# Small experts multiply gate and up tiles in float32 on two halves of the array's columns, with eleven raw tiles

## The chip, the core and the metric

One core of one Trainium2 chip runs the whole program. The time is device microseconds (us) from the first to the last instruction of the program and what lies around it, a median of three runs. TensorE is called PE here, its weight loads PEld, VectorE DVE, ScalarE ACT, GpSimd POOL, and SP is the engine that issues nearly all DMAs.

## What is computed

The reference is a decoder trunk of two layers over 272 tokens of width 1024. Each layer mixes tokens (attention, a state-space branch and a short convolution) and then applies a channel mixer. The second layer's channel mixer is the part that matters here, a choice of two experts out of eight for each of the last 256 tokens:

```
def swiglu(t, w_gu, w_down):
    gate, up = jnp.split(t @ w_gu, 2, axis=-1)
    return (jax.nn.silu(gate) * up) @ w_down

logits = (t @ router_w + router_b)
top_val, top_idx = lax.top_k(logits, TOP_K)          # TOP_K = 2, N_EXPERTS = 8
top_w = jax.nn.softmax(top_val, axis=-1)
for e in range(N_EXPERTS):
    out = out + combine[:, e:e + 1] * swiglu(t, w_gu[e], w_down[e])
```

Each expert has gate and up weights of 1024 x 7168 and down weights of 3584 x 1024, all float32. Every expert's weights are read once from memory, however many tokens it has.

## The kernel before

**Tiles and steps.** An expert is done in 7 steps (`NJ`); step `j` takes 512 columns of gate and of up and 512 rows of down. The weights of a step are six raw tiles of 128 x 2048 float32, 1 MB each: two of gate, two of up, two of down. `expert_units` (line 1230) lists these units in the order in which they are loaded and used: gate 0 and 1 of step i, down 0 and 1 of step i-2, up 2 and 3 of step i. Gate and up are both called `up` in the code. There are 8 x 7 x 6 = 336 units.

**Raw tiles.** `load_unit` (line 1244) issues the DMA of the next unit on SP into the next of ten raw tiles, which come from two pools A and B in the order of `RAWS`. A tile can be written again when all readers of the unit before it in that tile are done. The DMAs stand in one queue, in the order of the units. The first eleven units are asked for ahead of the loop, and each call of `make_low(k)` asks for one more.

**Splitting.** To multiply float32 with the array's faster one-pass format (float32r), a unit is split into a high and a low part: `make_high` (line 1270) copies it on ACT with rounding, `make_low` (line 1282) subtracts the high part from the raw tile on DVE. Both are called ahead of use, the high part two units ahead and the low part one.

**Two kinds of expert.** The tokens of an expert stand in up to 128 slots, as high and low parts. An expert with more than 64 tokens (`full`) multiplies high x high, low x high and high x low: twelve matmuls of 512 columns for each unit. An expert with at most 64 tokens ("small" below) puts the 64 high parts and the 64 low parts of its tokens side by side into the 128 columns of the array, and needs eight. PE, ACT and DVE each read the flag of the expert into a register, and branch on it.

**The unsplit tile.** In a small expert, units of gate with q = 0 are not split (`direct`, line 1260, for all steps but the very first): PE multiplies the raw tile itself in float32 (line 1303), four matmuls, each of which the hardware executes as two passes, so that the trace has two records for one. `make_high` and `make_low` stand behind a branch for these units and are skipped there; in a full expert the branch goes the other way and the unit is split.

**Order.** The loop of `experts` (line 1319) is laid out by hand in six slots for a step. `pair(k)` (line 1375) multiplies two units on even slots: gate in slot 0, down in slot 2, up in slot 4. `evict`, `turn` (four transposes on PE), `second`, `total`, `silu`, `product` and `inner` turn gate and up into the rows that the down units multiply two steps later. `rows`, `combine` and `add` bring the expert's result to the output. In odd experts `dispatch` builds the inputs of the next two. PE accumulates into one bank of its output memory (PSUM) for a pair, 128 partitions x 512 columns.

The attention and the state-space branch of the first part have float32 matmuls of 64 columns whose outputs go to the partitions 0 to 63 and 64 to 127 of one bank in turn (lines 534, 648, 650 and 652):

```
for j in range(2):
    nc.tensor.matmul(py[64 * j : 64 * j + 64, l0:T], x4[:, ki, j, :],
                     seg[:, j, c0 : c0 + T - l0], start=ki == 0, stop=ki == 2)
```

Of the kernel before, what the change touches and what calls it, by code (L numbers as in the profile page):

```python
# [21 lines left out]
P = 128  # L22
D_MODEL = 1024
KD = 8
# [7 lines left out]
N_EXPERTS = 8  # L32
FF_EXPERT = 3584
NJ = FF_EXPERT // 512
XORDER = (8, 9, 10, 11, 0, 1, 2, 3, 4, 5, 6, 7)
WARM = 12
WA, WB = 8, 10
RAWS = "ABBABABAAB"
HALF = 64
ALPHA = (2 * DEPTH) ** 0.25  # L40
EPS = 1e-5
# [20 lines left out]
def rr(ap):  # L62
    return ap.bitcast(F32)
# [38 lines left out]
class Builder:  # L102
    def __init__(self, ctx, tc, A, out):
        self.ctx, self.tc, self.nc, self.A, self.out = ctx, tc, tc.nc, A, out
        pool = lambda name, bufs, **kw: ctx.enter_context(tc.tile_pool(name=name, bufs=bufs, **kw))
        self.cp = pool("const", 1)
        self.rawp = pool("raw", RAWS.count("A"))
        self.rawps = {"A": self.rawp}
# [1121 lines left out]
    def expert_units(self):  # L1230


        self.steps = [(e, j) for e in range(N_EXPERTS) for j in range(NJ)]
        n = len(self.steps)
        self.units = []
        for i in range(n):
            self.units += [("up", i, 0), ("up", i, 1)]
            if i > 1:
                self.units += [("down", i - 2, 0), ("down", i - 2, 1)]
            self.units += [("up", i, 2), ("up", i, 3)]  # L1240
        self.units += [("down", i, q) for i in (n - 2, n - 1) for q in range(2)]
        self.raws, self.high, self.low, self.whole, self.fulls = [], [], [], {}, {}

    def load_unit(self):
        if len(self.raws) == len(self.units):
# [14 lines left out]
    def direct(self, k):  # L1260


        kind, i, q = self.units[k]
        e = self.steps[i][0]
        return kind == "up" and q == 0 and i > 0 and self.fulls[e] is not None

    def if_split(self, k, engine):
        return self.tc.If(self.fulls[self.steps[self.units[k][1]][0]][engine] > 0) if self.direct(k) else nullcontext()
# [23 lines left out]
    def products(self, full, units):  # L1292


        mm = self.nc.tensor.matmul
        whole = lambda x: (x[:, 0, :], x[:, 1, :])
        both = lambda x: (x.rearrange("p a n -> p (a n)")[:, 0 : 2 * P : 2],)

        def some(cases, unsplit):
            for k, parts, first, last in units:  # L1300
                if unsplit and self.direct(k):
                    for i, (ps, x) in enumerate(parts):
                        mm(ps, rr(both(x)[0]), self.raws[k][:, i * 512 : i * 512 + 512], start=i in first, stop=i in last)  # L1303
                    continue
                for i, ((ps, x), hv) in enumerate(zip(parts, self.high[k])):
                    for c, a in enumerate(cases(x)):
                        mm(ps, a, hv, start=i in first and c == 0, stop=False)  # L1307
                for i, ((ps, x), lv) in enumerate(zip(parts, self.low[k])):
                    mm(ps, cases(x)[0], lv, start=False, stop=i in last)  # L1309

        if full is None:
            some(whole, False)
        else:
            with self.tc.If(full[mybir.EngineType.PE] > 0) as case:
                some(whole, False)
            with case.Else():
                some(both, True)

    def experts(self, base, first):
# [4 lines left out]
        nc = self.nc  # L1324
        V, ACT = nc.vector, nc.scalar.activation
        steps = self.steps
        fulls, ps, g, f2, py, y2, sums = self.fulls, {}, {}, {}, {}, {}, {}
# [47 lines left out]
        def pair(k):  # L1375
# [16 lines left out]
                                  (0, 1) if j == 0 and q == 0 else (), (2, 3) if j == NJ - 1 and q else ()))  # L1392
            self.products(fulls[e], units)

        def rows(e, hf, part):

            if part == 0:
                y2[e, hf] = self.tmp("sel", [P, 2, 512], F32R, bufs=1)
                ACT(y2[e, hf][:, 0, :], py[e][hf], AF.Copy)
            else:  # L1400
                V.tensor_sub(y2[e, hf][:, 1, :], py[e][hf], rr(y2[e, hf][:, 0, :]))
# [18 lines left out]
        with self.tc.manual_schedule():  # L1420
            value(0)
            value(1)
            k = 0
# [5 lines left out]
            for i, (e, j) in enumerate(steps):  # L1429

                done = e - 1 if j == 1 and e else None
                after = e - 1 if j == 2 and e else None
                if j == 2:
                    value(e + 1)
                if e % 2 and j == 2 and e + 1 < N_EXPERTS:
                    nxt = self.dispatch(e + 1)
                for slot in range(6):
                    idle = slot in (2, 3) and i < 2

                    if slot == 2 and i:  # L1440
                        turn(i - 1, 1)
                    if slot == 4:
                        turn(i, 0)
                    if slot == 2 and j == 2 and e % 2 and e + 1 < N_EXPERTS:
                        next(nxt)
                    busy = slot % 2 == 0 and e % 2 and e + 1 < N_EXPERTS and (j > 2 or j == 2 and slot == 4)
                    if busy:
                        next(nxt, None)

                    if not idle:  # L1450
                        self.make_high(k + 2)
                    if busy:
                        next(nxt, None)
                    if slot == 0 and i:
                        evict(i - 1, 1)
                        silu(i - 1)
                    if slot == 2:
                        evict(i, 0)
                    if slot == 3 and i:
                        second(i - 1, 1)  # L1460
                    if slot == 5:
                        second(i, 0)
                    if slot == 4 and i:
                        product(i - 1)
                        inner(i - 1, 0)
                    if slot == 5 and i:
                        inner(i - 1, 1)
                    if after is not None and slot in (0, 2):
                        add(after, slot // 2)
                    if after is not None and slot == 0:  # L1470
                        rows(after, 1, 0)
                    if done is not None and slot == 4:
                        rows(done, 0, 0)
                    if idle and i and not base:
                        ACT(self.oa[:, slot - 2, :], self.oa[:, slot - 2, :], AF.Copy, scale=ALPHA)
                    if not idle:
                        self.make_low(k + 1)
                    if after is not None and slot == 0:
                        rows(after, 1, 1)
                    if done is not None and slot == 4:  # L1480
                        rows(done, 0, 1)
                    if slot == 3 and i:
                        total(i - 1, 1)
                    if slot == 5:
                        total(i, 0)
                    if idle:
                        continue

                    if slot % 2 == 0:
                        pair(k)  # L1490
                    if slot == 5 and done is not None:
                        combine(done, 0)
                    if slot == 1 and after is not None:
                        combine(after, 1)
                    k += 1
            last = len(steps) - 1
# [15 lines left out]
        e = N_EXPERTS - 1  # L1512
# [186 lines left out]
```

## Time and profile before

| | us |
|---|---|
| median of 3 runs (1835.1 to 1837.23) | 1835.48 |
| profiled execution | 1838.82 |
| its span, first to last instruction | 1837.1 |
| first layer, mixer and router, until PE begins with the experts | about 893 |
| experts, until the last matmul of the last pair | about 922 |
| after it: last sums, normalization, output | about 21 |

The profile lists busy time of each engine over the span: PE 97%, PEld 84%, DVE 81%, ACT 67%, POOL 16%. A busy PE is not PE at its peak. Busy shares are an average over stages with different limits, so the stage of the experts is read by itself. The eight experts follow each other as one full (from 893 us), two small (1007.6 to 1217.3), two full (1217.3 to 1471.4), two small (1471.4 to 1681.1) and one full; the matmuls of line 1303 show the small ones, since only they run it. Their 224 records are 28 unsplit tiles of four matmuls with two records each.

### The profile page before, as it was taken

What the parts mean: (1) busy time and instruction counts of PE and PEld (TensorE: products, weight loads), DVE (VectorE), ACT (ScalarE), POOL (GpSimd) and SP (SyncE); (2) the same over time, 40 slices, a digit from 0 to 9 for tenths busy, and PEclk for the clock granted to TensorE, in tenths of its full rate; (3) what the DMA queues carried; (4) which work ended last, traced back from release to release, by engine and by line L of the source; (5) the groups of instructions that cost most, each with busy time, mean ns of one, the idle gap of its engine ahead of it and who ended that gap; (6) DMA issues with size and microseconds to landing.
All of it is one profiled execution on the core that took longest, in us unless ns stands there. A gap on an engine that the chain in (4) does not pass through costs nothing.

```text
span 1837.1 us, 28288 instructions
## 1 busy us (share of the span) xinstructions
PE 1780.4 (97%) x10759; PEld 1547.5 (84%) x10759; DVE 1481.0 (81%) x1676; ACT 1238.0 (67%) x1623; POOL 292.8 (16%) x379
## 2 busy tenths in 40 slices
PE   8999999999999999999899999999999999999996
PEld 7989999899998999998787777787888877777784
DVE  7796675865568877675798889999899888999996
ACT  5565564654446665554687788897877778889783
POOL 6115731600032109530000000000000000000000
PEclk8999999999999999999899999999999999999998
DMA  5445545445454445557399999999888899999990
GB/s 206 158 139 174 183 148 179 136 153 170 150 189 167 158 157 187 194 184 275 127 367 377 373 387 403 419 419 412 337 351 339 362 362 402 408 419 419 419 385 30
DMA packets 74839, 497.12 MB, mean 271 GB/s; under 512 B 9340, under 2 KB 10924, under 8 KB 17324
## 3 DMA queue, kind: packets, MB, share of 16 engines
q1 hardware_dynamic: 69200, 486.64, 69.0%
q10 hardware_dynamic: 5468, 8.15, 1.5%
q8 instruction: 114, 1.87, 0.4%
q14 instruction: 57, 0.47, 0.1%
HBM read 493.65 MB, written 1.10 MB: 269 GB/s over the span
## 4 chain that ended last, share of the span: by engine, by line
PE 87%; DVE 8%; issue 1%; POOL 1%; ACT 1%; DMA 1%; SPq 0%; DVEq 0%; ACTq 0%; POOLq 0%
PE ps_mm L1307 15%; PE ps_mm L198 12%; PE ps_mm L200 12%; PE ps_mm L199 12%; PE ps_mm L1309 9%; PE ps_acc L1307 8%; PE ps_mm L1303 5%; PE ps_acc L1309 5%; DVE wlo L1288 3%; PE ps_tp L1344 2%; DMA raw<-in_q 1%; PE ps_acc L534 1%; PE ps_acc L607 1%; DVE w L172 1%; PE ps_tp L1407 1%
## 5 line engine op out<-in xcount | busy, mean ns | idle before, releaser
L1288 DVE TENSOR_TENSOR wlo<-raw,mhi 128x2048 fp32r<-128x2048 f32 x308 | 692.2, 2279 | 17.1 <-ACT mhi L1277 5.7
L1277 ACT ACTIVATE mhi<-raw 128x2048 fp32r<-128x2048 f32 x308 | 581.9, 1909 | 25.2 <-PE ps_acc L1309 15.7
L172 DVE TENSOR_TENSOR w<-raw,w 128x1024 fp32r<-128x1024 f32 (+2 forms) x260 | 320.2, 1232 | 164.0 <-ACT w L171 162.8
L198 PE MATMUL ps_mm<-HL,w 128*128 128x272 f32 (+2 forms) x1344 | 393.1, 292 | 1.0 <-DVE t L393 0.7
L200 PE MATMUL ps_mm<-HL,w 128*128 128x272 f32 (+2 forms) x1344 | 386.2, 287 | 0.0
L199 PE MATMUL ps_mm<-HL,w 128*128 128x272 f32 (+2 forms) x1344 | 384.5, 286 | 1.1 <-DVE HL L377 1.1
L171 ACT ACTIVATE w<-raw 128x1024 fp32r<-128x1024 f32 (+2 forms) x260 | 265.2, 1020 | 120.9 <-PE ps_mm L200 89.0
L1307 PE MATMUL ps_mm<-mhi,xe 128*128 128x512 f32 x1224 | 329.8, 406 | 0.1
L1307 PEld LDWEIGHTS ps_mm<-mhi,xe 128*128 128x128 f32 x1224 | 227.7, 190 | 57.6 <-issue 13.5
L198 PEld LDWEIGHTS ps_mm<-HL,w 128*128 128x128 f32 x1344 | 253.1, 188 | 4.1 <-issue 1.4
L199 PEld LDWEIGHTS ps_mm<-HL,w 128*128 128x128 f32 x1344 | 253.4, 189 | 1.7 <-DVE HL L377 1.3
L200 PEld LDWEIGHTS ps_mm<-HL,w 128*128 128x128 f32 x1344 | 253.0, 188 | 0.2 <-DVE w L172 0.2
L1309 PE MATMUL ps_mm<-wlo,xe 128*128 128x512 f32 x780 | 213.1, 394 | 4.1 <-DVE wlo L1288 4.1
L1309 PEld LDWEIGHTS ps_mm<-wlo,xe 128*128 128x128 f32 x780 | 148.5, 191 | 38.0 <-DVE wlo L1288 7.2
L1307 PE MATMUL ps_acc<-mhi,f 128*128 128x512 f32 x672 | 177.8, 399 | 0.1
L1593 POOL TENSOR_TENSOR raw<-raw,gb 128x768 f32<-128x768 f32 x1 | 1.8, 1802 | 978.4 <-ACT raw L1583 978.4
L1307 PEld LDWEIGHTS ps_acc<-mhi,f 128*128 128x128 f32 x672 | 123.5, 190 | 23.6 <-issue 0.2
L1309 PE MATMUL ps_acc<-wlo,f 128*128 128x512 f32 x448 | 122.1, 394 | 0.0
L492 POOL TENSOR_SCALAR seg<-b,ctm 128x16 f32<-128x16 f32 (+3 forms) x96 | 101.1, 1071 | 41.8 <-PE ps_acc L534 21.2
L1303 PE MATMUL ps_mm<-raw,xe 128*128 128x512 f32 x224 | 101.0, 593 | 0.0
L1309 PEld LDWEIGHTS ps_acc<-wlo,f 128*128 128x128 f32 x448 | 85.7, 192 | 18.1 <-DVE wlo L1288 0.2
L1338 ACT ACTIVATE e<-ps_mm 128x512 f32<-128x512 f32 x112 | 67.0, 598 | 50.0 <-PE ps_mm L1309 49.9
(362 smaller groups left out, 2570.7 us busy)
## 6 DMA issues: line engine op xcount, KB each, us to landing
raw<-in_up SPq DMA_DIRECT2D x224, 1024.0 KB, 10.1
raw<-in_down SPq DMA_DIRECT2D x110, 1024.0 KB, 11.5
raw<-in_g SPq DMA_DIRECT2D x24, 1024.0 KB, 4.9
raw<-in_q SPq DMA_DIRECT2D x12, 1024.0 KB, 5.5
raw<-in_x SPq DMA_DIRECT2D x12, 1024.0 KB, 4.9
raw<-in_dg SPq DMA_DIRECT2D x11, 1024.0 KB, 5.0
raw<-in_du SPq DMA_DIRECT2D x11, 1024.0 KB, 4.8
raw<-in_dd SPq DMA_DIRECT2D x16, 704.0 KB, 4.1
```

The costliest lines, as they stand in the source:

```text
L171: pin(nc.scalar.activation(hv, src, AF.Copy))
L172: pin((eng or nc.vector).tensor_sub(lv, src, rr(hv)))
L198: nc.tensor.matmul(ps, h, a, start=first and k == 0, stop=False)
L199: nc.tensor.matmul(ps, h, b, start=False, stop=False)
L200: nc.tensor.matmul(ps, lo, a, start=False, stop=last and k == kn - 1)
L492: nc.gpsimd.tensor_scalar(seg[:, j, c0 : c0 + T - l0], ab[:, j, l0:T], self.ctm[:, ki, hd : hd + 1], 0.0, OP.subtract, OP.min)
L1277: d = self.nc.scalar.activation(hi[:, v], self.raws[k][:, v], AF.Copy)
L1288: self.nc.vector.tensor_sub(lo[:, v], self.raws[k][:, v], rr(self.whole[k][:, v]))
L1303: mm(ps, rr(both(x)[0]), self.raws[k][:, i * 512 : i * 512 + 512], start=i in first, stop=i in last)
L1307: mm(ps, a, hv, start=i in first and c == 0, stop=False)
L1309: mm(ps, cases(x)[0], lv, start=False, stop=i in last)
L1338: ACT(g[i, half], ps.pop((i, half)), AF.Copy)
```

## The change

In small experts all four gate and up units of a step are multiplied unsplit, not only the first (`direct`). The stationary operand is no longer 64 high and 64 low parts in 128 columns of the array, but the 64 exact float32 sums of both (`unsplit` adds them on DVE once for an expert into a new tile `rows`). Each matmul fills 64 columns: row blocks 0 and 2 of a unit go to the first half of the columns and the partitions 0 to 63 of the bank, row blocks 1 and 3 to the second half and the partitions 64 to 127. The two halves hold partial sums over different row blocks; `second` and `total` add them, as they added the high and the low parts before. Down units, and full experts, are computed as before; in full experts all four gate and up units now have the branches on ACT and DVE. `RAWS` has eleven tiles, the new one in pool B. For its room, the part of the on-chip memory that is kept aside for DMA descriptors is cut to 1024 bytes a partition.

```
-RAWS = "ABBABABAAB"
+RAWS = "ABBABBABAAB"
@@ direct
-        kind, i, q = self.units[k]
-        e = self.steps[i][0]
-        return kind == "up" and q == 0 and i > 0 and self.fulls[e] is not None
+        kind, i, _ = self.units[k]
+        return kind == "up" and i > 0 and self.fulls[self.steps[i][0]] is not None
@@ products
                 if unsplit and self.direct(k):
-                    for i, (ps, x) in enumerate(parts):
-                        mm(ps, rr(both(x)[0]), self.raws[k][:, i * 512 : i * 512 + 512], start=i in first, stop=i in last)
+                    kind, i, q = self.units[k]
+                    rows = self.rows[self.steps[i][0]]
+
+                    for i, (ps, _) in enumerate(parts):
+                        c = i % 2 * HALF
+                        mm(ps[c : c + HALF], rows[:, q % 2 * 4 + i, :], self.raws[k][:, i * 512 : i * 512 + 512],
+                           start=bool(first) and i < 2, stop=bool(last) and i > 1)
                     continue
@@ experts
+        def unsplit(e):
+
+            if e < N_EXPERTS and not base:
+                x = rr(self.slots[e][0])
+                self.rows[e] = self.tmp("xf", [P, KD, HALF], bufs=2)
+                V.tensor_add(self.rows[e], x[:, :, 0, 0::2], x[:, :, 1, 0::2])
...
+                    if i == 0 and slot == 2:
+                        unsplit(0)
+                    if j == NJ - 1 and slot == 4:
+                        unsplit(e + 1)
@@ kernel
-    nc = _bacc.Bacc("TRN2", target_bir_lowering=False, num_devices=1)
+    nc = _bacc.Bacc("TRN2", target_bir_lowering=False, num_devices=1, dynamic_dma_scratch_size=1024)
```

## Rows read from the trace of the kernel before

**Rows 1.** The page's first part: busy us, share of the span, instructions.
```profile
PE 1780.4 (97%) x10759; PEld 1547.5 (84%) x10759; DVE 1481.0 (81%) x1676; ACT 1238.0 (67%) x1623; POOL 292.8 (16%) x379
PE 87%; DVE 8%; issue 1%; POOL 1%; ACT 1%; DMA 1%; SPq 0%; DVEq 0%; ACTq 0%; POOLq 0%
```
**Rows 2.** Windows: length, busy PE, PEld, DVE, ACT, POOL, clock, DMA share, GB/s.
```profile
1007.60:1217.30 209.70, 204.49 (x854) 151.93 (x853) 196.40 (x150) 172.37 (x175) 0.00 (x0) 1.00 0.98 397
1217.30:1471.40 254.10, 250.37 (x1157) 204.41 (x1156) 229.58 (x166) 200.50 (x188) 0.00 (x0) 1.00 0.91 366
1471.40:1681.10 209.70, 204.44 (x855) 151.83 (x854) 196.37 (x150) 172.51 (x175) 0.00 (x0) 1.00 0.98 400
```
**Rows 3.** Timeline of PE over one step of a small expert (start, us, ...).
```profile
1176.48 3.60 PE L1303 MATMUL ps_mm<-raw,xe 128*128 128x512 f32 x8
...
1181.79 0.60 PE L1344 MATMUL ps_tp<-ident,e 128*128 128x128 f32 x4
1182.14 1.18 PE L1307 MATMUL ps_acc<-mhi,f 128*128 128x512 f32 x4
...
1185.95 0.60 PE L1344 MATMUL ps_tp<-ident,e 128*128 128x128 f32 x4
1186.30 1.18 PE L1307 MATMUL ps_mm<-mhi,xe 128*128 128x512 f32 x4
...
1190.11 3.60 PE L1303 MATMUL ps_mm<-raw,xe 128*128 128x512 f32 x8
```
**Rows 4.** Timeline of PE, float32 matmuls of 64 columns in the attention.
```profile
99.27 0.60 PE L650 MATMUL ps_acc<-seg,b 128*64 128x256 f32 x4
99.70 0.39 PE L652 MATMUL ps_acc<-seg,b 128*64 128x128 f32 x4
```
**Rows 5.** Timeline of PE around such matmuls in the state-space branch.
```profile
172.97 0.29 PE L200 MATMUL ps_mm<-HL,w 128*128 128x272 f32 x1
173.19 1.00 PE L534 MATMUL ps_acc<-seg,b 128*64 128x272 f32 x12
174.12 0.39 PE L198 MATMUL ps_mm<-HL,w 128*128 128x272 f32 x1
174.35 0.29 PE L199 MATMUL ps_mm<-HL,w 128*128 128x272 f32 x1
174.48 0.29 PE L200 MATMUL ps_mm<-HL,w 128*128 128x272 f32 x1
```
**Rows 6.** Windows again: twenty us of a small expert, late.
```profile
1200.00:1220.00 20.00, 20.00 (x86) 15.47 (x85) 19.82 (x14) 19.76 (x19) 0.00 (x0) 1.00 1.01 419
```
**Rows 7.** Raw tiles from issue to landing: windows 985 to 1007, 1190 to 1217.
```profile
DMA to landing us min/median/max: 5.0/9.9/10.9
DMA to landing us min/median/max: 12.5/16.6/19.2
```
**Rows 8.** Windows: five whole steps of a full expert.
```profile
1374.90:1462.60 87.70, 87.31 (x400) 71.06 (x399) 80.27 (x55) 68.82 (x61) 0.00 (x0) 1.00 0.87 348
```
**Rows 9.** Waits from 1000 to 1220 us (total us, times, longest).
```profile
PE ps_tp L1344 <- DVE oa L1413: 2.0, 2, 1.6
DVE e L1352 <- ACTq L1275: 2.0, 3, 0.9
```
**Rows 10.** Waits of SP's queue from 900 to 1800 us.
```profile
SPq L1253 <- DVE wlo L1288: 612.2, 204, 15.2
SPq L1253 <- PE ps_mm L1307: 53.0, 10, 6.0
```
**Rows 11.** Groups of instructions in the late small expert and, second, all experts.
```profile
L1288 DVE TENSOR_TENSOR wlo<-raw,mhi 128x2048 fp32r<-128x2048 f32 x37 | 83.0, 2284 | 0.0
L1359 DVE TENSOR_TENSOR e<-e,e 128x512 f32<-128x512 f32 x56 | 38.7, 692 | 1.9
```
**Rows 12.** Windows: granted clock where PE has little to do.
```profile
345.00:350.00 5.00, 2.33 (x19) 2.11 (x17) 4.31 (x7) 3.35 (x7) 4.05 (x5) 1.00 0.63 210
350.00:357.00 7.00, 6.09 (x17) 4.61 (x18) 5.83 (x9) 4.54 (x9) 2.81 (x4) 0.54 0.25 64
1040.00:1060.00 20.00, 18.08 (x74) 12.62 (x73) 19.37 (x20) 14.39 (x19) 0.00 (x0) 1.00 0.97 369
```

More of the change, by code (lines that the diff above doesn't have):

```diff
@@ L1241, in expert_units @@
         self.units += [("down", i, q) for i in (n - 2, n - 1) for q in range(2)]
-        self.raws, self.high, self.low, self.whole, self.fulls = [], [], [], {}, {}
+        self.raws, self.high, self.low, self.whole, self.fulls, self.rows = [], [], [], {}, {}, {}
     def load_unit(self):
```

## The prediction, made before the change was run

> **What bounds the kernel now.** I read the page's first part and the chain that ended last first: PE is busy 97% of the span and 87% of the chain is PE [rows 1]. That says little by itself, because the experts have two kinds of stages, so I cut the experts into stretches with the windows view [rows 2]. Two small experts take 209.7 us each time, two full ones 254.1 us. In both, PE is busy for nearly the whole stretch, but the other resources differ. In the small stretch DVE is busy 196.4 of 209.7 us and the DMAs move 397 GB/s; late in it DVE has 19.82 of 20 us and the DMAs 419 GB/s, with a share of 1.01 of what they can do [rows 6]. No stretch of the trace moves clearly more, so I take 419 GB/s as the most that this core gets. A raw tile is 1024 KB, so it costs 1.0486 MB / 419 GB/s = 2.503 us of the DMAs, and a step of six tiles 15.02 us. A step of a small expert takes 13.63 us in steady state [rows 3], from one line 1303 to the next. PE and DVE eat tiles faster than the DMAs bring them, out of the stock in the raw tiles. In the full stretch the DMAs move 366 GB/s and wait for PE; there the stock is filled again. So three things stand close together in the small experts: PE, DVE and the DMAs, and the full experts are PE's alone.
>
> A rule of the Trainium skill speaks against reading 419 GB/s as steady. DMA: Bandwidth & Descriptors, section Specifications, gives 358 GB/s as the limit of the memory for one core. The windows here show 419 [rows 6], so the measurement decides; by the page's figure, as an estimate, a tile would cost 2.93 us and the small experts could only get slower.
>
> **The size of the stock.** In the stretch from 1007.6, 397 GB/s x 209.7 us = 83.3 MB = 79.4 tiles arrive, and 84 (two experts x 42) are used. So the stock gives 4.6 tiles. The landing times agree: from issue to landing it is 9.9 us (median) just before the stretch and 16.6 us (up to 19.2) at its end [rows 7], at 2.503 us a tile 4 tiles in the queue against 7.
>
> **PE's part of the change.** The step in [rows 3] splits into the first gate/up pair with one unsplit tile, 1181.79 - 1176.48 = 5.31 us; the down pair, 1185.95 - 1182.14 = 3.81; the second gate/up pair, 1190.11 - 1186.30 = 3.81; and two groups of transposes at 0.35. The split tile of a pair costs about 1.9, so the unsplit one costs 3.4 us: eight records of 512 columns at 0.43 each. After the change a gate/up pair has eight matmuls, 16 records, of 64 columns of the array. If they run one after another that is 16 x 0.43 = 6.9 us, if two at a time 3.44. The trace has the same form of work: in line 650, j = 0 and j = 1 alternate between the halves of the columns, and four records of 256 columns take 99.70 - 99.27 = 0.43 us [rows 4]. One record of 256 on its own would take half of 0.43 by the unsplit tiles, so four would take 0.86. They do run two at a time, and I take 3.44.
>
> Going into this form and out of it costs something. In [rows 5] line 534 starts 0.22 us after the last whole-array matmul, where 272 columns take 0.12 to 0.13 (174.35 to 174.48): 0.10 in. Out, line 199 follows line 198 after 0.23 instead of 0.13, and line 198 itself starts about 0.13 late (the twelve records, 2 x (272 + 144 + 16) columns a half, take 0.72 to 0.75 of the 0.93 us, with 0.05 at their start). So 0.33 a pair, between 0.1 and 0.5. The Trainium skill (TensorEngine Tiling, section Tiling Modes) says that a change of the tiling mode drains the engine, without a price; the rows give one, and by them the drain is small here. A gate/up pair becomes 3.44 + 0.33 = 3.77 us and a step 2 x 3.77 + 3.81 + 0.70 = 12.05, that is 1.58 less than 13.63. Over the 14 steps of a stretch PE saves 22.1 us. PE's idle time in a stretch, 209.7 - 204.5 = 5.2 us, stands mostly behind DVE (line 1344 behind line 1413, [rows 9]), and can go too: PE's floor is 182 to 188 us a stretch.
>
> **ACT and DVE.** Of the 35 units that a small expert splits, 21 go away (84 in the four): each 2.28 us on DVE [rows 11] and somewhat less on ACT. DVE keeps two low parts a step and small work, about 7 of 15 us, and bounds nothing there. `unsplit` adds one addition of 128 x 512 an expert, 0.69 us by the nearest form [rows 11]; eight are 5.5 us, hidden behind DVE's slack. In full experts DVE is busy 80.3 of 87.7 us in five steps [rows 8], a slack of 1.5 us a step, which covers it; without that cover it is 2.8 us in the four. Three more units a step have branches on ACT and DVE. A branch is sequencer work that passes while the engine still runs the instruction before; where it doesn't, the trace shows waits of 0.7 us on average and 0.9 at most (line 1352 behind line 1275, three times in a small stretch, [rows 9]). I take 0 in the full experts, with bounds 0 and 0.6 us a step x 27 steps = 16 us.
>
> **The DMAs' part.** With PE at 182 to 188 us and DVE far below, a stretch is bounded by the DMAs: t = (84 - stock) x 2.503. At today's 4.6 tiles t = 198.7. The eleventh raw tile adds up to one tile of stock. Against it, SP can issue the load of a gate/up tile only after PE is done with the unit before it in that tile, and no longer after DVE. SP's queue shows both releasers already [rows 10]: 204 waits for DVE's line 1288, 3.0 us each, and 10 for PE's line 1307 in full experts, 5.3 us each. All later loads stand behind the waiting one, and ACT's and PE's next reads behind them. In a full expert a step takes 17.5 us (87.7 / 5), so a hold longer by two tiles still leaves about 6 tiles x 2.9 us for a load that lands in 5 to 11 us: hidden. At the start of a small stretch it costs about the tile that was gained. At the end of the stretch the small experts wait for data, so the queue can fill to what the work doesn't hold: 11 less 3 or 4 in use, 7 or 8 tiles, up to one more than now. I take 5.5 tiles, between 4 and 7: t = 78.5 x 2.503 = 196.5 us, between 192.7 and 200.2. PE has 8 to 14 us to spare there, 0.3 to 0.5 us for each of the 28 gate/up pairs.
>
> So a stretch saves 209.7 - 196.5 = 13.2 us (9.5 to 17), both 26.4 us (19 to 34), although PE's work falls by 44. The full experts, which begin with a stock a tile lower, are PE's at 2.9 us a tile against 2.5: no change. The profiled execution was 1838.8 us, 1.7 more than its span and 3.3 above the median; the sum gives 1812.4 for such an execution and 1809.1 for the median.
>
> **The rivals.** *The halves don't overlap.* Then a gate/up pair costs 6.9 + 0.33 = 7.2 us, a step 18.9, 5.3 more than now, in 28 steps 148; the 10 us of waits behind DVE go: 1835 + 138 = 1973. For it: the rows show 256 and 272 columns, the change has 512, and both halves would then draw full raw tiles at once. Against it: [rows 4, 5] have the same type, the same halves and one bank, and four records in the time of two.
>
> *The full experts get slower.* The mechanism is the branches on DVE: four of six units a step behind one instead of one. It decides once three extra branches cost DVE more than its 1.5 us a step [rows 8]. At 1.0 us each, near the longest wait seen, with no cover, 27 steps x (3.0 - 1.5) = 41 us: 1809 + 41 = 1850, slower. For it: DVE is the second engine there. Against it: it is hidden for the unit that has a branch now, and waits behind branches are rare in the trace.
>
> *PE's clock falls while PE waits for tiles.* After a stretch in which PE was busy 2.33 of 5 us, the granted clock was 0.54, half speed (1.2 GHz) most of the time, for 7 us; at 18.08 of 20 it stayed at 2.4 GHz [rows 12]. After the change PE is busy 12 of 15 us once the stock is gone, about 6 steps at the end of each stretch. If in each the clock halved for some 7 us, PE would lose 3.5 us of the 3.0 that it has: 6 us in all; if it stayed low through them, 12 x (24 - 15) = 108: 1917. The Trainium skill (TensorE: Matmul & The Clock Gate, section HAM oscillation — how this bites in real kernels) describes this, a clock that falls again and again in DMA waits between short runs of matmuls; no row here shows it for waits as short as these. Late PE work piles up tiles and makes PE busy again, so I hold the long case unlikely.
>
> *Entering and leaving the halves is dearer,* 1.2 us a pair instead of 0.33: PE's floor 207 to 212 a stretch, no gain, 1830 to 1840.
>
> *No stock limit.* If more tiles stood in stock than I count, PE's floor would hold: 2 x 24 us, 1787.
>
> **How the numbers follow.** Forecast 0.74, 1809 (1801 to 1817 by the stock, to 1826 with the branches' bound and short drops of the clock); no overlap 0.06; full experts slower 0.08; clock 0.04; dearer switching 0.05; no stock limit 0.03. The range from 1793 to 1826 holds the forecast and half of the neighbours. A measurement of this kernel can tell 0.2%, 3.7 us, from no change. Faster: forecast, no stock limit and some of the three in between, 0.84; same 0.05; slower 0.11, of it 0.06 from the first rival and the rest from the full experts and the switching.
>
> **What would show it.** Windows from the first small expert to the next full one: about 196 us, DMAs at 419 GB/s throughout, PE with idle time whose releaser is the DMA of raw. The gate/up matmuls as 128*64, starting in twos, a pair near 3.8 us. 84 fewer of lines 1277 and 1288. Full stretches as long as now. A pair near 7 us, a full stretch over 260 us, a clock below 1.00 or DMAs below 415 GB/s in the small stretches would each prove a step wrong.

## The result and the profile after

| | before | after |
|---|---|---|
| median | 1836.36 us | 1814.18 us |
| lowest to highest | 1835.10 to 1838.69 | 1813.55 to 1818.60 |
| profiled execution | 1838.82 | 1813.66 |
| its span | 1837.1 | 1811.9 |

The ratio is 0.9886, with a 95% interval from 0.9871 to 0.9900: 22.2 us less, where 26.4 were forecast. The forecast was 1809.0, within 1793 to 1826. Comparisons use fast executions alone; one execution of `e4_ten` below, at a mean clock of 0.593, took 2681.62 us.

From the page of after, the busy time of the engines and two groups of instructions, which answer to [rows 1] and [rows 11]:

```profile
PE 1737.7 (96%) x10759; PEld 1433.1 (79%) x10759; DVE 1307.0 (72%) x1600; ACT 1097.0 (61%) x1539; POOL 291.0 (16%) x379
L1287 DVE TENSOR_TENSOR wlo<-raw,mhi 128x2048 fp32r<-128x2048 f32 x224 | 506.2, 2278 | 102.9 <-ACT mhi L1276 49.0
L1306 PE MATMUL ps_mm<-raw,xf 128*64 128x512 f32 x896 | 201.1, 597 | 0.0
```

PE did 43 us less, DVE 174 and ACT 141, and the span is 25.2 us shorter. Four tenths of what PE saved are not in the time. The chain of work that ended last can't be used here: in after it breaks off when it covers some 9% of the span. The windows between the same two events as in [rows 2] tell where the time went. A small stretch goes from the first pair with an unsplit tile to the first full pair after it; then come two full experts, the second small stretch, and the last expert with the tail. Columns as in [rows 2], after:

```profile
1003.85:1200.17 196.32, 183.84 (x854) 96.84 (x853) 107.89 (x108) 101.04 (x131) 0.00 (x0) 0.98 1.01 417
1200.17:1457.50 257.33, 251.34 (x1159) 204.02 (x1157) 230.73 (x168) 201.17 (x190) 0.00 (x0) 1.00 0.93 369
1457.50:1654.67 197.17, 184.07 (x853) 96.53 (x852) 107.86 (x108) 100.94 (x131) 0.00 (x0) 0.98 1.01 415
1654.67:1811.90 157.23, 137.81 (x614) 108.98 (x612) 136.08 (x103) 110.53 (x102) 4.46 (x2) 0.97 0.74 303
```

Set against [rows 2] (and 156.0 us for the last part before; the small stretches of [rows 2] begin 0.2 us ahead of that pair):

- up to the first small stretch: 3.8 us less
- first small stretch: 209.7 to 196.3, 13.4 less
- full experts: 254.1 to 257.3, 3.2 more
- second small stretch: 209.7 to 197.2, 12.5 less
- last expert and tail: 156.0 to 157.2, 1.2 more. Its last transfer takes 2.1 less of it, 5.5 us instead of 7.6 from its issue to the end of the span, so the expert itself 3.3 more

The sum is the 25.2 us of the spans. The small stretches show what now sets their time: the DMAs' share is 1.01 over the whole of them, at 417 and 415 GB/s where [rows 2] have 397 and 400, and PE and DVE have idle time (PE 12.5 us, DVE 88). The prediction looked for PE idle behind the DMA of raw, and no wait of PE's in this stretch is put down to a DMA. It is ACT that waits for tiles, and PE waits behind ACT and DVE. Waits from 1003.85 to 1200.17 (total us, times, longest):

```profile
ACT mhi L1276 <- DMA raw<-in_down: 22.1, 6, 5.6
PE ps_tp L1348 <- ACT e L1342: 3.5, 3, 1.7
PE ps_tp L1348 <- DVE oa L1424: 2.8, 2, 1.6
```

One steady step of a small expert, timeline of PE (start and length in us), which answers to [rows 3]:

```profile
1140.92 0.60 PE L1348 MATMUL ps_tp<-ident,e 128*128 128x128 f32 x4
1141.45 7.09 PE L1306 MATMUL ps_mm<-raw,xf 128*64 128x512 f32 x32
1148.47 0.66 PE L1348 MATMUL ps_tp<-ident,e 128*128 128x128 f32 x4
1148.88 1.18 PE L1311 MATMUL ps_acc<-mhi,f 128*128 128x512 f32 x4
...
1152.69 0.60 PE L1348 MATMUL ps_tp<-ident,e 128*128 128x128 f32 x4
1153.21 7.09 PE L1306 MATMUL ps_mm<-raw,xf 128*64 128x512 f32 x32
```

The step takes 1152.69 - 1140.92 = 11.77 us, 13.63 before. The up pair of one step and the gate pair of the next stand back to back, 32 records in 7.09 us, so a pair costs 3.5.

### The profile page after: what moved, and what is told of

The parts are those of the page before. It is cut to its first block, busy times and chain, and to the rows that moved or that the text cites. A ratio compares the mean times of both kernels' runs of the same rounds, so it can differ in the third digit from the quotient of the medians.

```text
span 1811.9 us, 28892 instructions
## 1 busy us (share of the span) xinstructions
PE 1737.7 (96%) x10759; PEld 1433.1 (79%) x10759; DVE 1307.0 (72%) x1600; ACT 1097.0 (61%) x1539; POOL 291.0 (16%) x379
## 3 DMA queue, kind: packets, MB, share of 16 engines
q8 instruction: 114, 1.87, 0.4%
## 5 line engine op out<-in xcount | busy, mean ns | idle before, releaser
L1287 DVE TENSOR_TENSOR wlo<-raw,mhi 128x2048 fp32r<-128x2048 f32 x224 | 506.2, 2278 | 102.9 <-ACT mhi L1276 49.0
L1276 ACT ACTIVATE mhi<-raw 128x2048 fp32r<-128x2048 f32 x224 | 424.1, 1904 | 79.3 <-DMA raw<-in_down 47.7
L1311 PE MATMUL ps_mm<-mhi,xe 128*128 128x512 f32 x888 | 225.3, 395 | 0.1
L1306 PE MATMUL ps_mm<-raw,xf 128*64 128x512 f32 x896 | 201.1, 597 | 0.0
L1311 PEld LDWEIGHTS ps_mm<-mhi,xe 128*128 128x128 f32 x888 | 164.2, 188 | 37.7 <-ACT mhi L1276 1.6
L1306 PEld LDWEIGHTS ps_mm<-raw,xf 128*64 128x64 f32 x896 | 60.8, 137 | 112.5 <-issue 110.9
L1313 PE MATMUL ps_mm<-wlo,xe 128*128 128x512 f32 x444 | 121.3, 394 | 2.2 <-DVE wlo L1287 2.2
```

The source lines that it names most:

```text
L1276: d = self.nc.scalar.activation(hi[:, v], self.raws[k][:, v], AF.Copy)
L1287: self.nc.vector.tensor_sub(lo[:, v], self.raws[k][:, v], rr(self.whole[k][:, v]))
L1306: mm(ps[c : c + HALF], rows[:, q % 2 * 4 + i, :], self.raws[k][:, i * 512 : i * 512 + 512], start=bool(first) and i < 2, stop=bool(last) a ...
```

## The experiments

All times are medians of two to five executions, eleven for `e9_before11`, and one alone for `e5_one_half`; "after" is 1814.18, and the kernel before beside them 1836.2 to 1836.7. The length of a stretch is given from the transposes of the first small expert's first step to those of the first full one's: 207.9 us in both stretches before, 197.9 and 198.8 after.

### Do the halves run together, and does the order matter?

`e1_order` changes the order in which the four blocks are issued, so that two in a row go to the same half:

```diff
-                    for i, (ps, _) in enumerate(parts):
+                    for i in (0, 2, 1, 3):
+                        ps = parts[i][0]
```

> The four row blocks of an unsplit tile are multiplied in the order 0, 2, 1, 3 instead of 0, 1, 2, 3, so that two matmuls (four records) in a row go to the same half of the columns. Nothing is left out. If the two halves overlap because neighbouring matmuls go to different halves, this order loses most of it: with records started strictly in order a gate/up pair would take about 12 turns of 0.43 instead of 8, 5.2 us instead of 3.6, a stretch of two small experts about 235 us instead of 196, and the time about 1890. If nothing overlaps in this order, 6.9 us a pair and about 1985. Rival: the queue finds the overlap in any order; then the time stays at 1814.

Measured: 1815.91, ratio 0.9887 (0.9869 to 0.9905), no different from after. Its timeline shows the same 32 records in the same time:

```profile
1154.64 0.60 PE L1349 MATMUL ps_tp<-ident,e 128*128 128x128 f32 x4
1155.16 7.14 PE L1307 MATMUL ps_mm<-raw,xf 128*64 128x512 f32 x32
```

My theory, that a matmul behind another on its own half holds up the one for the other half, fell. The records start two at a time every 0.43 us in both kernels, 0.01 us apart in after and 0.01 to 0.06 in `e1_order`. They don't carry the half, so they don't say how the two for different halves come together.

`e5_one_half` puts all four blocks on the first half. The second half gets one matmul of zeros in each pair, so that what reads it finds zeros; every product is still computed.

```diff
-                        c = i % 2 * HALF
-                        mm(ps[c : c + HALF], rows[:, q % 2 * 4 + i, :], self.raws[k][:, i * 512 : i * 512 + 512],
-                           start=bool(first) and i < 2, stop=bool(last) and i > 1)
+                        mm(ps[:HALF], rows[:, q % 2 * 4 + i, :], self.raws[k][:, i * 512 : i * 512 + 512],
+                           start=bool(first) and i == 0, stop=bool(last) and i > 2)
+                        if first and i == 0:
+                            mm(ps[HALF:], self.zero, self.raws[k][:, :512], start=True, stop=True)
```

> All four row blocks of an unsplit tile go to the first half of the columns; the second half gets one matmul with a stationary operand of zeros in each pair, so that the sum is the same. This takes the overlap of the halves away and leaves the rest. If the overlap is what makes a gate/up pair 3.6 us, a pair now takes 16 x 0.43 = 6.9 us, a stretch about 182 + 28 x 3.4 = 277 us instead of 198, and the time is about 1972. Rival: the halves matter little, because the records of a 64-column matmul are shorter or the DMAs hide it; then it stays under 1840.

Measured: 1969.77, in a single execution. Its timeline of PE:

```profile
1149.48 7.03 PE L1307 MATMUL ps_mm<-raw,xf 128*64 128x512 f32 x16
1156.44 0.66 PE L1351 MATMUL ps_tp<-ident,e 128*128 128x128 f32 x4
...
1175.07 0.66 PE L1351 MATMUL ps_tp<-ident,e 128*128 128x128 f32 x4
```

Sixteen records now take 7.03 us where after needs 3.5, and a step 18.63 instead of 11.77: the overlap of the halves is worth 3.43 us a pair. The zeros run beside the others and cost nothing that shows. So the first rival of the prediction was a real danger, with the price that it gave (1973): without the second half the kernel is 7% slower than before. The mechanism of the change, two halves at once, is shown by this pair of runs.

### What bounds the small experts now?

Two kernels give PE more work and the DMAs none: a matmul with zeros on each half, added to every pair, 256 columns wide in `e2_load256`, 512 in `e3_load512`.

```diff
+                        if i == 1 and q % 2:
+                            for c in (0, HALF):
+                                mm(ps[c : c + HALF, :256], self.zero, self.raws[k][:, :256], start=False, stop=False)
```

> Each gate/up pair of a small expert gets one more matmul of 64 columns on each half, 256 wide, with a stationary operand of zeros, so that the result is the same: two records at a time, 0.43 us of PE a pair, 12 us in each stretch of 28 pairs. If the DMAs bound the stretch (196 us, PE busy 187 of 200), the added work falls mostly into PE's idle time: 0 to 3 us a stretch, 1814 to 1820. Rival: PE still bounds the small experts; then 24 us in all, 1838.

> The same added matmuls 512 wide: 0.86 us of PE a pair, 24 us in each stretch. If the DMAs bound the stretch with about 10 us of PE to spare, 14 us of it come through in each, about 1843. Rival: PE bounds, 48 us in all, 1862. If PE had far more to spare than counted, under 1825.

Measured: 1818.87 (ratio 0.9903, 0.9888 to 0.9918) and 1826.91 (0.9948, 0.9933 to 0.9963). With 0.43 us a pair, 12 us in a stretch of 28 pairs, the stretches are 198.7 and 199.7, almost those of after: PE had that much room. The time is 4.7 us above after's, a fifth of the 24 us that were added: 1.7 in the profiled stretches, and 2.2 in the full experts between them, where the clock fell once for 3.4 us in this execution. With 0.86 us, 24.1 in a stretch, every step of the second small expert takes 13.48 but the third (16.33), the last ones too, and the stretch 205.7. In late steps of `e3_load512` PE no longer waits at all, and all its waits in the first stretch come to 3.1 us:

```profile
1151.53:1205.00 53.47, 53.47 (x256) 26.48 (x255) 28.89 (x27) 27.73 (x33) 0.00 (x0) 1.00 1.01 419
```

So PE sets the time there, and PE's own floor in after is 205.7 - 24.1 = 181.6 us: 16 us below the 198 of the DMAs. The larger load cost 16 us less than I had expected, since I had put the spare at some 10.

`e4_ten` takes the eleventh raw tile away again, `e8_twelve_hi3` has twelve, with three buffers for the high parts instead of four to make the room:

```diff
-RAWS = "ABBABBABAAB"
+RAWS = "ABBABABAAB"        (e4_ten)
+RAWS = "ABBABBABABAB"      (e8_twelve_hi3, with pool("ehi", 3))
```

> The changed kernel with ten raw tiles as before. If the stretches of small experts are bounded by the DMAs and the stock in the raw tiles, each tile of stock is worth 2.5 us in each of the two stretches: 5 us, about 1819. Rival: the eleventh tile only makes up for the longer hold or does nothing to the time, because PE or another wait bounds: 1813 to 1815.

> Twelve raw tiles, with the room taken from the high parts (three tiles instead of four). If the stock sets the small stretches, one more tile is worth 2.5 us in each: about 1809, if the full experts keep their 17.55 us a step. If the high part, called two units ahead, has to wait for its tile there, the full experts get slower; a wait of 0.5 us a unit would be 70 us over the four. Rival: a twelfth tile does nothing because the small stretches are bounded elsewhere: 1814 or more.

Measured: 1819.98 (ratio 0.9907, 0.9891 to 0.9922) and 1812.14 (0.9863, 0.9847 to 0.9880). The first stretch, between the same events as above, first of `e4_ten`, then of `e8_twelve_hi3`:

```profile
1005.97:1204.84 198.87, 184.23 (x854) 97.00 (x853) 107.87 (x108) 100.91 (x131) 0.00 (x0) 0.98 1.01 417
```
```profile
1009.71:1203.52 193.81, 182.74 (x854) 96.20 (x853) 107.87 (x108) 101.92 (x132) 0.00 (x0) 0.99 1.01 417
```

With ten, eleven and twelve raw tiles the stretch takes 198.87, 196.32 and 193.81 us. Each tile takes 2.5 us off, the time in which one tile arrives (1.0486 MB / 417 GB/s = 2.51). In the second stretch it is 198.81, 197.17 and 193.79 us, 5.0 for the two tiles, but 1.6 and 3.4 for each. That is the stock at work: what lies ready when the stretch begins needn't arrive in it. In `e8_twelve_hi3` only part of the 5 us of two stretches is in the time; the span of its profiled execution is that of after, since the clock was at half for 13.7 us before its experts and for 3.4 in after (more on that in the last experiment).

`e9_before11` gives the kernel before the eleventh tile and nothing else of the change:

```diff
-RAWS = "ABBABABAAB"
+RAWS = "ABBABBABAAB"
```

> The kernel before with eleven raw tiles and the smaller room for DMA descriptors, and nothing else. If PE and DVE bounded its small experts (13.6 us a step against 15.0 for the DMAs, with a stock that is not used up), the tile brings nothing: 1834 to 1837. Rival: the stock bounded them already; then 5 us, about 1831.

Measured: 1836.30, ratio 0.9995 (0.9986 to 1.0005). The tile is worth 5.8 us with the new matmuls and nothing without. Before, PE and DVE set the time ([rows 2, 6]), and a larger stock helps only who waits for tiles.

### Which of the matmuls count?

`e6_gate` takes only the gate pair unsplit, on two halves; the up pair is split as before. `e10_one` takes only the one tile that was unsplit before, on two halves.

```diff
-        return kind == "up" and i > 0 and self.fulls[self.steps[i][0]] is not None
+        return kind == "up" and q < 2 and i > 0 and self.fulls[self.steps[i][0]] is not None
...
+        return kind == "up" and q == 0 and i > 0 and self.fulls[self.steps[i][0]] is not None
```

> Only the gate pair of a small expert's step is unsplit on the two halves; the up pair is split as in the kernel before, 3.81 us on PE instead of 3.63, with four low parts a step on DVE. If the DMAs bound the stretches and PE, ACT and DVE have time to spare, unsplitting the up pair is worth nothing: 1811 to 1816; as DVE frees the up tiles earlier than PE does, the stock can be a tile larger, and it may even be up to 5 us faster. Rival: the gain comes from the work that is taken off PE, ACT and DVE in proportion; then a good part of it goes, and the time is 1820 to 1827.

> Only the first gate tile of a step is unsplit, as in the kernel before, but on the two halves of the columns; eleven raw tiles. PE gets 1.3 us a step, DVE still makes five low parts a step, about 13.6 us. If DVE stood close behind PE in the kernel before, the late small experts keep their 13.6 us a step and only the odd ones, where dispatch lengthens PE's step, gain: about 8 us a stretch, 1818 to 1823. Rival: DVE did not count; then PE's saving alone takes the stretch to the DMAs' bound and the time is 1812 to 1815.

Measured: `e6_gate` 1812.81 (ratio 0.9870, 0.9854 to 0.9887), as fast as after: its steps take 12.07 us, still below the 15.0 in which six tiles arrive, and its stretches 199.4 and 198.1. Half of the change brings all of its gain. On PE an unsplit pair (3.5) is hardly less than a split one (3.8, [rows 3]); what the second one saves is DVE's and ACT's, who had ceased to matter.

`e10_one` 1828.56 (ratio 0.9950, 0.9936 to 0.9964), 8 us below before and some 6 above what I had expected. A late part of its small stretch, and PE's waits in it:

```profile
1127.00:1185.00 58.00, 52.76 (x233) 36.99 (x232) 57.05 (x43) 48.19 (x47) 0.00 (x0) 1.00 1.01 419
```
```profile
PE ps_mm L1313 <- DVE wlo L1287: 3.2, 4, 0.8
```

The unsplit tile takes PE 1.87 us instead of 3.44, but the step fell only from 13.63 to 13.36, with DVE busy 57.05 of 58.00 us. DVE stood right behind PE, as [rows 6] had shown with 19.82 of 20. So PE's gain needs DVE's: a second tile unsplit takes 2.28 us a step from DVE, and then the DMAs are next.

### Does the clock, or the hold-up that brings it down, cost anything?

In after PE's granted clock falls once in each small stretch, in the third step of the second expert. Windows over it, columns as in [rows 12]:

```profile
1124.00:1132.00 8.00, 5.83 (x25) 1.92 (x21) 2.06 (x4) 4.08 (x5) 0.00 (x0) 1.00 1.01 420
1132.00:1139.00 7.00, 5.69 (x15) 4.22 (x16) 6.82 (x7) 2.11 (x3) 0.00 (x0) 0.51 1.02 421
1139.00:1146.00 7.00, 7.00 (x35) 3.54 (x36) 2.07 (x4) 3.82 (x5) 0.00 (x0) 1.00 1.01 417
```

and the timeline of PE and of ACT there (in brackets the idle time before the instruction and what ended it):

```profile
1131.37 0.50 PE L1418 MATMUL ps_tp<-sel,st 128*128 128x512 f32 x1 [2.04 <-ACT sel L1410]
1134.96 1.11 PE L1348 MATMUL ps_tp<-ident,e 128*128 128x128 f32 x4 [1.21 <-DVE oa L1424]
```
```profile
1127.92 1.91 ACT L1276 ACTIVATE mhi<-raw 128x2048 fp32r<-128x2048 f32 x1 [5.57 <-DMA raw<-in_down]
1130.73 0.59 ACT L1410 ACTIVATE sel<-ps_acc 128x512 fp32r<-128x512 f32 x1
```

ACT waits 5.57 us for a down tile that hasn't arrived. Its copy of the finished expert's rows (line 1410), which needs no tile, stands behind that wait; PE waits for the copy, and the step takes 20.49 us. PE was busy 5.83 of 8 us, and then ran at 0.51, half speed (1.2 GHz), for 7 us. `e7_rows_first` issues the copy ahead of the high part:

```diff
+                    if after is not None and slot == 0:
+                        rows(after, 1, 0)
+                    if done is not None and slot == 4:
+                        rows(done, 0, 0)
...
-                    if after is not None and slot == 0:
-                        rows(after, 1, 0)
-                    if done is not None and slot == 4:
-                        rows(done, 0, 0)
```

> In the steps in which an expert's result is taken over, ACT copies it (rows) ahead of the high part of the next unit instead of behind it, so that the copy no longer stands behind a wait for a DMA. In the changed kernel step 2 of the late small experts takes 20.5 us, PE's clock falls to half in it, and step 2 of the full expert that follows takes 23.4 instead of 22.3. If the DMAs bound the small stretch, the shorter step and the clock there bring nothing, and at most 1 to 2 us come back in the full experts: 1811 to 1815. Rival: the late step and the clock cost what they show, 5 us in each stretch: 1803 to 1806.

Measured: 1815.29 (ratio 0.9885, 0.9869 to 0.9902): nothing gained. The step falls from 20.49 to 18.10, and the half speed from 6.8 to 3.4 us:

```profile
1126.00:1134.00 8.00, 6.34 (x28) 2.40 (x24) 4.24 (x4) 4.68 (x5) 0.00 (x0) 1.00 1.02 423
1134.00:1141.00 7.00, 6.04 (x26) 5.02 (x28) 4.84 (x6) 1.95 (x4) 0.00 (x0) 0.76 1.01 418
```

but the steps behind it go up from 11.77 and 13.47 to 12.66 and 14.94, and the stretch is 198.0, as in after (197.9). The DMAs were at 1.01 to 1.02 in these windows; PE's delay only let tiles pile up that it then ate faster. `e2_load256` says it from the other side: its clock stays at 1.00 through both stretches, and they are no shorter. The hold-up and the clock cost nothing as long as the DMAs bound the stretch.

### Can the parts be added up?

`e11_gate12` joins the gate pair alone with the twelve tiles and three high buffers of `e8_twelve_hi3`; `e12_gate12_warm` also raises the idle matmuls that PE does behind the router, ahead of the experts, from 10 to 22.

```diff
-WA, WB = 8, 10
+WA, WB = 8, 22             (e12_gate12_warm only)
```

> Only the gate pair unsplit, with twelve raw tiles and three tiles for the high parts. If both small gains add up (the gate pair alone 1812.8, the twelfth tile 2.5 to 3 us in each stretch), about 1808. Rival: with only three high tiles, the up pair's splitting waits, and the twelfth tile is used up by it: 1812 or more.

> The same with 22 instead of 10 of the matmuls that keep PE busy after the router's (their result is not used). In the traces the clock was at half speed for 3.4 to 13.7 us right before the experts, after PE had waited 3.6 us there for the router's last steps; that is worth up to some 5 us of PE and differs from run to run. If the wait sets the clock off, the added matmuls keep it at 2.4 GHz and the time falls by 2 to 5 us against the same kernel without them, with a narrower spread. Rival: the clock falls for another reason or the added matmuls delay the first inputs of the experts: no change or 1 to 2 us more.

Measured: 1813.19 (ratio 0.9875, 0.9860 to 0.9890) and 1812.30 (0.9869, 0.9854 to 0.9884). The gains don't add up in the time, where 1808 was expected. In the stretches of the profiled executions a good part of them does: `e11_gate12` has 196.5 and 197.6 us where `e6_gate` has 199.4 and 198.1, 3.4 us less in the two together where a tile was worth 5. But with three high buffers a steady step with a split up pair takes 12.64 instead of 12.07 us, and the two full experts between the stretches take 255.9 instead of 253.5. Of that, 0.9 us are in the third step of the second one, 20.82 instead of 19.92; `e8_twelve_hi3`, with three high buffers too, has 20.86 there. The rival, that the high buffers use the tile up, is borne out in part. The warm matmuls do what they were put there for. Windows ahead of the experts, of before, of after and of `e12_gate12_warm`:

```profile
880.00:890.00 10.00, 5.56 (x25) 5.04 (x25) 9.65 (x21) 6.84 (x9) 0.00 (x0) 0.66 0.38 115
```
```profile
880.00:890.00 10.00, 5.82 (x32) 5.41 (x32) 9.22 (x22) 7.79 (x10) 0.00 (x0) 0.83 0.47 140
```
```profile
880.00:890.00 10.00, 6.91 (x54) 6.16 (x53) 10.00 (x22) 6.84 (x9) 0.00 (x0) 1.00 0.38 114
```

At the end of the router's work the clock now stays at 1.00, but the time falls by 0.9 us only, where I had expected 2 to 5. The spread is narrower, 1811.75 to 1813.02 against 1811.80 to 1815.09, with four executions each. The three fastest kernels (1812.1, 1812.3, 1812.8) lie within 0.12% of after, and none of them beats it by more than these measurements can tell.

## Why the prediction was right, step by step

*The halves run two at a time: right.* 3.5 us a pair where 3.44 + 0.33 was taken, and `e5_one_half` shows the 3.43 that the overlap is worth. The 0.33 for entering and leaving was counted for each pair; two pairs stand back to back, so it is paid once in a step: 11.77 instead of 12.05 us.

*The DMAs bound the small stretch: right, and nearly to the size.* Forecast 196.5, measured 196.3 and 197.2. `e2_load256`, `e6_gate` and `e7_rows_first` each change PE's, DVE's or ACT's part of it and leave its length alone; `e4_ten` and `e8_twelve_hi3` change the stock and move it by 2.5 us a tile. At 417 GB/s 78.1 of the 84 tiles arrived in the first stretch, so the stock gave 5.9; 5.5 had been taken. With ten tiles it gave 4.9 and with twelve 6.9, so the eleventh brought its whole tile, and loads that wait for PE instead of DVE took nothing of it that shows. That the sum started from nearly the right stock was luck in part: 4.6 is what the kernel before ate of it, not what it had, since a larger stock brought that kernel nothing (`e9_before11`).

*How the queue fills: the mechanism was another.* I let it fill to what the work doesn't hold, 7 or 8 tiles. It filled to 8, but for another reason. SP's waits from 1160 to 1200 us, and the landing times of the loads issued then, which answer to [rows 10] and [rows 7]:

```profile
SPq L1253 <- DMA raw<-in_up: 22.6, 11, 2.1
SPq L1253 <- DMA raw<-in_down: 10.1, 5, 2.0
SPq L1253 <- DVE e L1356: 0.8, 3, 0.3
```
```profile
DMA to landing us min/median/max: 19.8/19.9/20.5
```

Sixteen waits for a DMA, and none for PE to be done with a tile. In the records, where the landing is known, each of these loads is issued 0.07 to 0.10 us after the load eight before it has landed: eight are open at once, 8 x 2.5 = 20.0 us, the landing time of that row. With ten, eleven and twelve tiles, and in the kernel before, none is issued sooner than 0.06 us after that landing. The records show why: the loads signal their landing by eight semaphores in turn, and ahead of nearly every one (333 of 338) SP waits for the very semaphore that the load will use, which the load eight before it used. The program sets this limit, and not the queue. It costs nothing, since the DMAs are never idle with eight open. So the stock that counts is that at the start of the stretch, not how full the queue gets at its end.

*PE's floor: 182 to 188 predicted, 182.2 found.* That is `e3_load512`'s stretch from pair to pair, the prediction's border, 206.3 less 24.1 (181.6 from transposes to transposes). The spare time was 14 to 15 us a stretch where 8 to 14 had been taken, so the gain in PE's work was a little further from the time than I said.

*The full experts "no change": this term was mis-sized.* They became 3.2 and 3.3 us longer, nearly all of it at their start. The first steps of the first full expert after a small one take 15.35, 16.04 and 23.43 us, 13.83, 15.70 and 22.28 before (from transposes to transposes, the first from those of the last small step). Windows from the first full pair over these steps, before and after; the second ends 0.6 us later in the work:

```profile
1217.30:1278.60 61.30, 59.06 (x275) 47.96 (x274) 59.39 (x46) 49.91 (x48) 0.00 (x0) 1.00 1.01 413
```
```profile
1200.17:1265.10 64.93, 60.42 (x278) 48.17 (x277) 62.16 (x47) 53.62 (x53) 0.00 (x0) 1.00 1.01 418
```

The DMAs are at 1.01 in both, and PE idles 4.5 us instead of 2.2. The small stretch had eaten the stock to nothing, and the first of these steps runs at the DMAs' pace, 15 us. The late tile reaches PE by way of ACT and DVE:

```profile
1197.89 1.91 ACT L1276 ACTIVATE mhi<-raw 128x2048 fp32r<-128x2048 f32 x1 [3.99 <-DMA raw<-in_up]
1200.40 0.69 DVE L1376 TENSOR_TENSOR f<-e,f 128x512 fp32r<-128x512 f32 x1 [3.50 <-ACT f L1374]
1203.35 1.19 PE L1313 MATMUL ps_mm<-wlo,xe 128*128 128x512 f32 x4 [1.10 <-DVE wlo L1287]
1235.71 0.73 PE L1418 MATMUL ps_tp<-sel,st 128*128 128x512 f32 x2 [1.70 <-DVE e L1356]
```

ACT waits for a tile, DVE waits behind ACT, and DVE begins the first low part of the full expert 0.8 us after PE has begun its pair; in the kernel before it began it 1.5 us ahead of the pair. DVE has little room to make that up (it is busy 62.16 of 64.93 us), so PE still waits for it in the third step, 1.70 us where it waited 0.53 before. These two waits are 2.3 of the 3.0 us that the three steps lose. I had compared PE's 2.9 us a tile with the DMAs' 2.5 over the whole expert, which is right from the fourth step on. `e3_load512` bears it out: its small stretch doesn't run dry, and its three steps take 14.77, 15.71 and 21.23, together as long as before's.

*The branches in the full experts: right.* A steady step takes 17.55 us in both kernels, and five steps have DVE busy for 79.9 of 87.6 us. The rival that priced them at 41 us fell.

*The clock: its rival was half right.* The clock did fall, for some 7 us in a stretch, but once, at the longest hold-up, and not in the steps behind it, in which PE was busy 48.84 of 55.05 us at 1.00. The Trainium skill (TensorE: Matmul & The Clock Gate, section HAM oscillation — how this bites in real kernels) has it fall again and again in DMA waits; waits as short as these did not bring that on here. The prediction had named a clock below 1.00 in the small stretches as a sign of a wrong step; it was 0.98, and what was wrong was only that it stays up. The 6 us that I gave it were none, as `e7_rows_first` and `e2_load256` show, because PE had at least 14 to spare.

*The price of a tile: right.* 2.503 us from 419 GB/s; the stretches moved 417 and 415 in the mean over nearly 200 us. The 358 GB/s of the Trainium skill (DMA: Bandwidth & Descriptors, section Specifications), half of what the page gives for two cores, is no limit for the one core that runs here.

*The sum.* The two small stretches gave 25.9 us (26.4 forecast), and the full experts took 6.5 back (0 forecast): 19.4. How it divides depends on the border: from transposes to transposes, the two stretches gave 9.9 and 9.1, and the two full experts between them take 255.7 after 255.8, since 1.5 us of the slow start then count to the stretch, and the faster first half of each stretch's first step (1.6 us) to the full expert ahead of it. Of the 25.2 between the profiled executions the rest, 5.8, stands in work that the change doesn't touch: before the experts, where the clock was at half for 13.7 us before and for 3.4 after, and in the last transfer. Over the profiled executions of this study, but for the one with the warm matmuls, the half speed there lasted 3.4 to 13.7 us, and its length did not go with the kernel: `e9_before11`, whose work up to there is that of before, had 3.4. The medians differ by 22.2, 2.8 more than the steps explain; whether that is the same chance or belongs to the change is open.

## What to carry to other kernels

Count the stretch and not the engine: PE, DVE and the DMAs stood within a few per cent of each other, so taking 43 us off one of them moved the bound to the next after 26, and a gain on PE alone (`e10_one`) stopped at DVE after 8. Where tiles are eaten faster than they arrive, the time is (tiles needed - tiles in stock at the start) x the time of one tile, and another buffer is worth about one tile (2.5 us here) in each such stretch, but nothing before that bound is reached. And a stretch that eats the stock to nothing hands a bill to the next one, 3.2 us here, because the engines that prepare its first tiles start late.

## What the runs showed of the hardware that I had not expected

- Float32 matmuls of 64 columns for the two halves overlap fully in either order of issue: 11.77 us a step with the halves in turn, 11.83 with two in a row for the same half.
- SP had eight loads open at once and no more, with ten, eleven or twelve tiles to be filled. The limit is the program's, which gives its loads eight semaphores in turn and waits for each before it is used again; what the queue itself would take is not shown.
- One core took 415 to 417 GB/s in the mean over nearly 200 us, and 417 to 423 over shorter ones.
- The same work behind the router ran at half clock for 3.4 us in one execution and for 13.7 in another; with 12 more idle matmuls of PE ahead of it the clock stayed at 1.00 in the one execution that was profiled.
